# Attention scores straight from q and k: one float32 matmul per block of queries in place of three matmuls of parts

## The chip, the cores and the metric

The kernel runs on one core of a Trainium2 chip, for one layer of a transformer-like encoder block over 256 tokens of width 2048. A core has a matrix engine (PE in the profile, with its weight loads listed apart as PEld), a vector engine (DVE), a scalar engine (ACT), a general engine (POOL), and a queue engine that issues most transfers (SP). The metric is the device time of one execution in microseconds (us), lower is better. A difference of about 0.2% is the least that a measurement of this kernel tells from no change.

## The reference, cut to what matters

The whole block is computed: RMSNorm, one input projection, windowed attention beside a Fourier mixer, output projection, a gated feed-forward part and a final RMSNorm. Only the attention's scores are touched by the change. For each of the 12 query heads (three share one key head) they are

```python
scores = jnp.einsum('bnqkgd,bnskd->bnkgqs', qb, kb).astype(jnp.float32)
scores = scores * (HEAD_DIM ** -0.5)
...
scores = scores + alibi[None, None]
scores = jnp.where(valid[None, :, None, None], scores, NEG_INF)
...
m = jnp.maximum(jnp.max(scores, axis=-1, keepdims=True), sink_b)
p = jnp.exp(scores - m)
```

The sequence has 256 positions and the window reaches 128 either way, so for one head the kernel forms the whole 256 x 256 table of scores, as two blocks of 128 queries against 256 keys, with a contraction over the 128 elements of a head.

## The kernel before, in words

All big products are done on numbers in a reduced float32 format (float32r, "F32R" in the code). To keep float32 accuracy an operand is split in two parts: `hi` is the operand rounded to that format (a copy on ACT), and `lo` is the remainder (a subtraction on DVE). A product is then three matmuls that add up in one accumulator: hi by hi, hi by lo, lo by hi. A matmul with plain float32 operands (tiles of type "F32") needs no split. The kernel has a few of those before the change: the warm-up matmuls `ps_warm`, the Fourier channel products `ps_y` (L652, matrices `G` by columns `uf`, 129 and 127 columns each), and four transposes `ps_t`.

The program is written out in order by hand: an engine does its instructions in the order in which the code issues them, with no reordering by a planner. The middle part of it, the stretch from 58 to 163 us of the profile, has 16 units, one for each head of `QK_ORDER` (k0, q0, q1, q2, k1, q3 and so on). A unit's own work is 32 matmuls of line L372 (`still_weights`) that make one head of q or k, transposed, from the weights and the activations `hT`. Around it the dictionaries `before`, `beside` and `behind` hang the small steps of earlier heads, by the distance to a head's own unit: one unit later its projection is read out (`qk_out`, then `qk_parts`), two units later `scores` puts its matmuls on PE ahead of that unit's projection and `scores_out` and `exps` follow on DVE and ACT, and further on the weights of the softmax are applied, turned and multiplied with v (`values`, L842). On DVE and ACT the small steps stand ahead of the split of a later unit's weight tile: L197 (`hi`, ACT, 1.9 us) and L205 (`lo`, DVE, 2.2 us), which a matmul needs two units later.

The steps that the change touches:

- `qk_out` copies half of the accumulator out (ACT, `tmp_q` or `tmp_k`, L725) and adds the other half (DVE, `add_q` or `add_k`, L727). For a key it also multiplies by `r1b`, the normalizing factor of each token (DVE, L729).
- `qk_parts` makes the operands of the scores. For a key: `kT`'s high part on ACT (L737) and low part on DVE (L738). For a query: both parts by `split_scaled`, with a scale that holds the head's slope (ACT L298, DVE L299).
- `scores` issues three matmuls of 256 columns for each of the two query blocks, L748, into one bank `ps_s`.

`ps_*` are accumulator banks, `kT` and `qT` the transposed keys and queries in on-chip memory. `scores` runs for all 12 query heads.

Of the kernel before, what the change touches and what calls it, by code (L numbers as in the profile page):

```python
# [8 lines left out]
F32 = mybir.dt.float32  # L9
F32R = mybir.dt.float32r  # L10
AF = mybir.ActivationFunctionType
ALU = mybir.AluOpType

P = 128
D = 2048
S = 256
# [41 lines left out]
def slopes():  # L58
    def pow2(n):
        start = 2.0 ** (-8.0 / n)  # L60
        return [start ** (i + 1) for i in range(n)]

    return pow2(8) + pow2(16)[0::2][: NH - 8]
# [57 lines left out]
def block_kernel(  # L121
# [19 lines left out]
    nc = tc.nc  # L141
    SL = slopes()
# [6 lines left out]
    def f32(ap):  # L149
        return ap.bitcast(F32)  # L150

    def bank(pool, name):
        return pool.tile([P, 512], F32, tag=pool.name, name=name)
# [92 lines left out]
    def u_part(k, o, n, m=1):  # L246

        rows = ux[k // 4][:, (k < 4) * U_HEAD :].rearrange("p (k c) -> p k c", k=4)
        return rows[:, k % 4 : k % 4 + m, o : o + n]
# [39 lines left out]
    ps = bank(dn, "ps_warm")  # L289
# [6 lines left out]
    def split_scaled(dst, src, g):  # L296

        nc.scalar.activation(dst[:, 0:S], src, AF.Copy, scale=g)  # L298
        nc.vector.scalar_tensor_tensor(  # L299
            dst[:, S : 2 * S], src, g, f32(dst[:, 0:S]), ALU.mult, ALU.subtract  # L300
        )
# [105 lines left out]
    for c in range(4):  # L407
        t = base.tile([P, 4, 512], F32R, tag=f"hT{c}", name=f"hT{c}")
        hT.append(t)
    ps_u = [bank(mm, f"ps_u{b}") for b in range(2)]  # L410
    for k in range(NK):
# [3 lines left out]
        n = 1 if c < 2 else 2  # L415
# [3 lines left out]
        if q % n == 0:  # L419
            w, h = u_part(k, 0, FW, n), hi[:, q : q + n, :]  # L420
# [3 lines left out]
        if k < 4:  # L424

            for p, w in enumerate([hi, hi, lo]):
                for b in range(2):
# [3 lines left out]
                        start=k == 0 and p == 0, stop=False,  # L431
# [9 lines left out]
    ph = pa.enter_context(tc.tile_pool(name="pa", bufs=1))  # L441
# [78 lines left out]
    r1b = ph.tile([P, S], F32, tag="r1b", name="r1b")  # L520
# [202 lines left out]
    def qk_out(kind, h, ps):  # L723
        tmp = ph.tile([P, S], F32, tag="tmp", name=f"tmp_{kind}{h}", bufs=2)
        nc.scalar.activation(tmp, ps[:, S : 2 * S], AF.Copy)  # L725
        add = ph.tile([P, S], F32, tag="add", name=f"add_{kind}{h}", bufs=2)
        nc.vector.tensor_tensor(add, ps[:, 0:S], tmp, ALU.add)  # L727
        if kind == "k":
            nc.vector.tensor_tensor(add, add, r1b, ALU.mult)  # L729
        st["add", kind, h] = add  # L730

    def qk_parts(kind, h):

        add = st.pop(("add", kind, h))
        t = ph.tile([P, 512], F32R, tag=f"{kind}T", name=f"{kind}T{h}", bufs=2)
        if kind == "k":
            nc.scalar.activation(t[:, 0:S], add, AF.Copy)  # L737
            nc.vector.tensor_tensor(t[:, S : 2 * S], add, f32(t[:, 0:S]), ALU.subtract)  # L738
        else:
            split_scaled(t, add, -1.0 / float(SL[h]))  # L740
        qk_sb[kind, h] = t

    def scores(h):
        ps = st["s", h] = bank(dn, f"ps_s{h}")
        qT, kT = qk_sb.pop(("q", h)), qk_sb["k", h // GQA]
        for b in range(2):
            for n, (qo, ko) in enumerate([(0, 0), (0, S), (S, 0)]):
                nc.tensor.matmul(  # L748
                    ps[:, b * S : (b + 1) * S],
                    qT[:, qo + b * P : qo + (b + 1) * P],  # L750
                    kT[:, ko : ko + S],
                    start=n == 0,
                    stop=n == 2,
                )

    def scores_out(h):

# [100 lines left out]
    for i in range(N_QK, N_OUT + 8):  # L858
        heads = {i - s: h for (kind, h), s in slot_of.items() if kind == "q"}
        new = [kh for kh, s in slot_of.items() if i - s == 1]  # L860
        for n, h in sorted(heads.items()):
            if n == values_at(h):
                at(before, i, values, h)
        if 4 in heads and heads[4] not in FLIPS:
            at(before, i, turn, heads[4])
        if 2 in heads:
            at(before, i, scores, heads[2])
        for kind, h in new:
            at(beside, i, lambda k=kind, h=h: qk_out(k, h, st.pop(("ps", k, h))))
        for n, h in sorted(heads.items()):  # L870
            if n == values_at(h) - 1 and h in FLIPS:
                at(beside, i, flip_parts, h)
        for kind, h in new:
            at(beside, i, qk_parts, kind, h)
        for n, h in sorted(heads.items()):
            if n == values_at(h):
                at(beside, i, values_out, h)
        if 3 in heads:
            at(beside, i, weigh, heads[3])
            if heads[3] in FLIPS:  # L880
                at(beside, i, flip_out, heads[3])
        if 4 in heads:
            at(beside, i, flip_in if heads[4] in FLIPS else turn_out, heads[4])
        if 2 in heads:
            at(beside, i, scores_out, heads[2])
        if 2 in heads:
            at(behind, i, exps, heads[2])
# [68 lines left out]
    for n, (c, kq) in enumerate(OUT_ORDER):  # L956
# [15 lines left out]
        if kq >= 2:  # L972
            part = "a" if kq == 2 else "f"
            ps = ps_a[c] if kq < 3 else ps_a[c, "f"]
# [345 lines left out]
    for q in range(OPEN):  # L1320
        kind, j = items[q]
        ps = bank(mm, f"ps_{kind}{j}")
# [29 lines left out]
    for n, it in enumerate(items):  # L1352
# [8 lines left out]
        if it[0] in ("gate", "val"):  # L1361
            kind, j = it
            ps = bank(mm, f"ps_{kind}{j}")
# [4 lines left out]
        if it[0] == "product":  # L1368
            kind, g, c, p = it
# [3 lines left out]
            elif end and p in ("P2", "N4"):  # L1373
                ps = joined[c, p] = bank(mm, f"ps_{p}{g}{c}")
                by_parts(ps, parts[p], *halves.pop(it), GROUPS[g][1], True, False)
            else:
                ps = bank(mm, f"ps_{p}{g}{c}")
# [5 lines left out]
        else:  # L1383
            kind, c = it
            hi, lo = halves.pop(up_index[n])
            if c < 2:
                ps = [joined.pop((c, p)) for p in ("P2", "N4")]
            else:
                ps = [bank(mm, f"ps_l{c}{b}") for b in range(2)]
# [172 lines left out]
```

## Time and profile before

| what | value |
|---|---|
| median of 3 runs | 933.79 us (933.52 to 934.1) |
| the profiled execution, its own time | 933.83 us |
| its span in the profile | 932.1 us |
| granted PE clock, mean | 0.998 |
| PE busy in the span | 923.2 us, 99% |
| DVE busy | 776.2 us, 83% |
| ACT busy | 543.6 us, 58% |

A row of a group names line, engine, operation and tiles (out<-in), the shape (partitions x elements), and a count; then the busy time and the mean duration of one. Matmuls overlap: one of 512 columns is listed with 389 ns, but the next one begins 0.23 us after it. So busy times of matmuls cannot be added up as time of the span. What can be added up is the chain that ended last: its pieces touch each other, so the length of a piece is what it takes of the span. A timeline row gives start and length of an instruction, or of several of one kind in a row ("x6"), from the first's start to the last's end.

### The profile page before, as it was taken

The page shows a single profiled execution, that of the slowest core. Times are in us where ns is not written, and L with a number is a line of the kernel's source. Part 1 is how long each engine was busy: PE and PEld are TensorE (multiplying, and loading weights), DVE is VectorE, ACT ScalarE, POOL GpSimd, SP SyncE. Part 2 cuts the span into 40 slices and gives each one's busy share as a digit, 9 for nine tenths or more (in the row PEclk, how much of TensorE's full clock was granted, in tenths as well). Part 3 has the DMA queues.
Part 4 walks back from the last instruction along what each step waited for, and adds up shares of the span by engine and source line. Part 5 has one row for each costly group of instructions (what it writes and reads, how often), then busy time and mean ns, then how long its engine had stood idle before and what let it go on. Part 6 is the DMA issues. An engine that isn't in the chain of part 4 may idle for free.

```text
span 932.1 us, 12883 instructions
## 1 busy us (share of the span) xinstructions
PE 923.2 (99%) x4973; PEld 799.9 (86%) x4973; DVE 776.2 (83%) x997; ACT 543.6 (58%) x689; POOL 62.8 (7%) x79
## 2 busy tenths in 40 slices
PE   9999999999999999999999999999999999999996
PEld 7888998888888888888888888888888888888885
DVE  7768998787768877898877997888978789989995
ACT  6756777546465655565555665555755556655553
POOL 0101111200000000000000000000000000000002
PEclk9999999999999999999999999999999999999999
DMA  9865777667777668788797769887787968779652
GB/s 361 331 225 158 249 241 215 201 198 269 230 274 256 203 207 256 242 274 263 229 299 251 240 209 298 223 260 233 268 240 244 306 221 269 237 238 272 203 180 91
DMA packets 59597, 225.16 MB, mean 242 GB/s; under 512 B 24465, under 2 KB 30225, under 8 KB 35984
## 3 DMA queue, kind: packets, MB, share of 16 engines
q1 hardware_dynamic: 54928, 194.72, 57.9%
q0 software_dynamic: 4464, 29.36, 17.0%
q8 instruction: 39, 0.64, 0.3%
q10 hardware_dynamic: 144, 0.26, 0.1%
q14 instruction: 22, 0.18, 0.0%
HBM read 216.98 MB, written 7.08 MB: 240 GB/s over the span
## 4 chain that ended last, share of the span: by engine, by line
PE 98%; DMA 0%; ACT 0%; DVE 0%; issue 0%; POOLq 0%; POOL 0%; ACTq 0%
PE ps_gate L372 25%; PE ps_val L372 25%; PE ps_q L372 7%; PE ps_P L1233 4%; PE ps_P L1234 4%; PE ps_P L1232 3%; PE ps_N L1233 3%; PE ps_N L1234 3%; PE ps_N L1232 3%; PE ps_k L372 2%; PE ps_a L357 2%; PE ps_a L355 2%; PE ps_a L356 2%; PE ps_s L748 1%; PE ps_o L842 1%; PE ps_ff L355 1%
## 5 line engine op out<-in xcount | busy, mean ns | idle before, releaser
L205 DVE TENSOR_TENSOR lo<-raw,hi 128x2048 fp32r<-128x2048 f32 (+2 forms) x133 | 295.0, 2221 | 28.3 <-ACT hi L197 28.0
L197 ACT ACTIVATE hi<-raw 128x2048 fp32r<-128x2048 f32 (+1 forms) x131 | 246.8, 1887 | 27.6 <-PE ps_a L356 10.8
L372 PE MATMUL ps_gate<-hU,hi 128*128 128x512 f32 x688 | 236.1, 389 | 0.0
L372 PE MATMUL ps_val<-hU,hi 128*128 128x512 f32 x688 | 236.1, 389 | 0.0
L372 PE MATMUL ps_gate<-hU,lo 128*128 128x256 f32 x688 | 189.9, 276 | 0.0
L372 PE MATMUL ps_val<-hU,lo 128*128 128x256 f32 x687 | 189.6, 276 | 0.0
L372 PEld LDWEIGHTS ps_gate<-hU,hi 128*128 128x128 f32 x688 | 129.2, 188 | 26.8
L372 PEld LDWEIGHTS ps_val<-hU,hi 128*128 128x128 f32 x688 | 129.2, 188 | 26.8
L372 PEld LDWEIGHTS ps_gate<-hU,lo 128*128 128x128 f32 x688 | 129.2, 188 | 1.3
L372 PEld LDWEIGHTS ps_val<-hU,lo 128*128 128x128 f32 x687 | 129.0, 188 | 1.3
L1013 ACT ACTIVATE ft_g<-ps_gate 128x256 f32<-128x256 f32 x43 | 16.5, 384 | 121.1 <-PE ps_gate L372 121.1
L1013 ACT ACTIVATE ft_v<-ps_val 128x256 f32<-128x256 f32 x43 | 16.5, 383 | 87.0 <-PE ps_val L372 87.0
L372 PE MATMUL ps_q<-hT,hi 128*128 128x512 f32 x192 | 65.0, 391 | 0.0
L1232 PE MATMUL ps_P<-hi_P,op_P 128*128 128x512 f32 x144 | 56.0, 389 | 0.0
L1233 PE MATMUL ps_P<-hi_P,op_P 128*128 128x512 f32 x144 | 56.0, 389 | 0.0
L1234 PE MATMUL ps_P<-lo_P,op_P 128*128 128x512 f32 x144 | 56.0, 389 | 0.0
L372 PE MATMUL ps_q<-hT,lo 128*128 128x256 f32 x192 | 51.2, 277 | 0.0
L1130 DVE TENSOR_TENSOR lo_N<-sumw,hi_N 128x2048 fp32r<-128x2048 f32 (+1 forms) x20 | 41.5, 2076 | 9.4 <-ACT hi_N L1129 9.2
L1232 PE MATMUL ps_N<-hi_N,op_N 128*128 128x512 f32 x108 | 42.0, 389 | 0.0
L1233 PE MATMUL ps_N<-hi_N,op_N 128*128 128x512 f32 x108 | 42.0, 389 | 0.0
L1234 PE MATMUL ps_N<-lo_N,op_N 128*128 128x512 f32 x108 | 42.0, 389 | 0.0
L372 PEld LDWEIGHTS ps_q<-hT,hi 128*128 128x128 f32 x192 | 35.2, 188 | 6.6
(415 smaller groups left out, 1592.4 us busy)
## 6 DMA issues: line engine op xcount, KB each, us to landing
raw<-in_w_up SPq DMA_DIRECT2D x86, 1024.0 KB, 6.6
raw<-in_w_in SPq DMA_DIRECT2D x20, 1024.0 KB, 5.4
raw<-in_w_out SPq DMA_DIRECT2D x16, 1024.0 KB, 5.1
sumw<-in_w_down POOLq DMA_DIRECT2D x16, 1024.0 KB, 8.6
raw<-in_w_down_late SPq DMA_DIRECT2D x4, 1024.0 KB, 6.8
raw<-in_w_down_last SPq DMA_DIRECT2D x4, 768.0 KB, 4.0
turnp<-flip SPq DMA_DIRECT2D x44, 64.0 KB, 1.9
flop<-turnp SPq DMA_DIRECT2D x11, 256.0 KB, 3.9
```

What stands on the lines that cost most here:

```text
L197: nc.scalar.activation(halves[i][0][:, s], raws[i][:, s], AF.Copy)
L205: nc.vector.tensor_tensor(lo[:, s], raws[i][:, s], f32(hi[:, s]), ALU.subtract)
L355: nc.tensor.matmul(ps, ah, wh, start=first and q == q0, stop=False)
L356: nc.tensor.matmul(ps, al, wh, start=False, stop=False)
L357: nc.tensor.matmul(ps, ah, wl, start=False, stop=last and q == q0 + len(kk) - 1)
L372: nc.tensor.matmul(ps[:, x], (hi, lo)[i][:, k * P : (k + 1) * P], hk(k)[:, x], start=n == 0 and k == 0, stop=n == len(order) - 1 and k == ...
L748: nc.tensor.matmul(ps[:, b * S : (b + 1) * S], qT[:, qo + b * P : qo + (b + 1) * P], kT[:, ko : ko + S], start=n == 0, stop=n == 2,)
L1013: nc.scalar.activation(tmp, ps[:, S : 2 * S], AF.Copy)
L1130: nc.vector.tensor_tensor(lo, src, f32(hi), ALU.subtract)
L1232: nc.tensor.matmul(ps, o[:, 0, p, :], hi[:, s], start=first and p == 0, stop=False)
L1233: nc.tensor.matmul(ps, o[:, 1, p, :], hi[:, s], start=False, stop=False)
L1234: nc.tensor.matmul(ps, o[:, 0, p, :], lo[:, s], start=False, stop=last and p == n - 1)
```

## The change

The high and low parts of q and k go. `qk_parts` now writes one plain float32 tile `t` of 256 columns: for a key it is the product of `add` with `r1b`, which stood in `qk_out` before (DVE, new line L735), and for a query it is `add` times the same scale as before (ACT, new line L737). `scores` issues one float32 matmul for each block of 128 queries in place of three float32r matmuls, new line L744. The results go to the same bank in the same shape, and nothing behind `scores` changes.

```diff
         add = ph.tile([P, S], F32, tag="add", name=f"add_{kind}{h}", bufs=2)
         nc.vector.tensor_tensor(add, ps[:, 0:S], tmp, ALU.add)
+        st["add", kind, h] = add
+
+    def qk_parts(kind, h):
+
+        add = st.pop(("add", kind, h))
+        t = ph.tile([P, 512], F32, tag=f"{kind}T", name=f"{kind}T{h}", bufs=2)[:, 0:S]
         if kind == "k":
-            nc.vector.tensor_tensor(add, add, r1b, ALU.mult)
-        st["add", kind, h] = add
-
-    def qk_parts(kind, h):
-
-        add = st.pop(("add", kind, h))
-        t = ph.tile([P, 512], F32R, tag=f"{kind}T", name=f"{kind}T{h}", bufs=2)
-        if kind == "k":
-            nc.scalar.activation(t[:, 0:S], add, AF.Copy)
-            nc.vector.tensor_tensor(t[:, S : 2 * S], add, f32(t[:, 0:S]), ALU.subtract)
+            nc.vector.tensor_tensor(t, add, r1b, ALU.mult)
         else:
-            split_scaled(t, add, -1.0 / float(SL[h]))
+            nc.scalar.activation(t, add, AF.Copy, scale=-1.0 / float(SL[h]))
         qk_sb[kind, h] = t
...
         for b in range(2):
-            for n, (qo, ko) in enumerate([(0, 0), (0, S), (S, 0)]):
-                nc.tensor.matmul(
-                    ps[:, b * S : (b + 1) * S],
-                    qT[:, qo + b * P : qo + (b + 1) * P],
-                    kT[:, ko : ko + S],
-                    start=n == 0,
-                    stop=n == 2,
-                )
+            nc.tensor.matmul(
+                ps[:, b * S : (b + 1) * S], qT[:, b * P : (b + 1) * P], kT, start=True, stop=True
+            )
```

On PE the scores of head 0 stand between the projection of head 2 (`ps_q`) and a Fourier product (`ps_y`). Before:

```order
L372 MATMUL ps_q_656<-hT_140,hi_566 128x512
L372 MATMUL ps_q_656<-hT_140,lo_567 128x256 x2
L748 MATMUL ps_s_719<-kT_644,qT_703 128x256 x6
L652 MATMUL ps_y_726<-uf_635,G_76 128x129
L652 MATMUL ps_y_726<-uf_635,G_77 128x127
L372 MATMUL ps_q_729<-hT_137,hi_647 128x512 x2
```

and after:

```order
L372 MATMUL ps_q_654<-hT_140,hi_566 128x512
L372 MATMUL ps_q_654<-hT_140,lo_567 128x256 x2
L744 MATMUL ps_s_716<-kT_643,qT_701 128x256 x2
L652 MATMUL ps_y_719<-uf_635,G_76 128x129
L652 MATMUL ps_y_719<-uf_635,G_77 128x127
L372 MATMUL ps_q_722<-hT_137,hi_645 128x512 x2
```

Six instructions of 256 columns became two of the same width, at the same place among the others.

On DVE the one step that moves is the multiplication of a key by `r1b`. Here it is for the third key head, beside the parts `pt` of the softmax weights of an earlier head (`flip_parts`). Before:

```order
L205 TENSOR_TENSOR lo_1201<-raw_971,hi_1200 128x2048
L727 TENSOR_TENSOR add_k_1261<-ps_k_1134,tmp_k_1259 128x256
L729 TENSOR_TENSOR add_k_1261<-add_k_1261,r1b 128x256
L833 TENSOR_TENSOR pt_1265<-flop_1100,pt_1264 128x256 x2
L738 TENSOR_TENSOR kT_1270<-add_k_1261,kT_1270 128x256
L299 SCALAR_TENSOR_TENSOR cat_1273<-ps_o_1212,vec,cat_1273 128x256
```

and after:

```order
L205 TENSOR_TENSOR lo_1171<-raw_952,hi_1170 128x2048
L727 TENSOR_TENSOR add_k_1227<-ps_k_1105,tmp_k_1225 128x256
L825 TENSOR_TENSOR pt_1230<-flop_1075,pt_1229 128x256 x2
L735 TENSOR_TENSOR kT_1235<-add_k_1227,r1b 128x256
L299 SCALAR_TENSOR_TENSOR cat_1237<-ps_o_1182,vec,cat_1237 128x256
```

The multiplication went behind the two subtractions of `pt`, to the place where the subtraction for `kT`'s low part stood, and that subtraction is gone. No transfer is issued at another place than before.

## The prediction

> **What bounds the kernel now.** The page comes first: its busy times, and then the chain that ended last.
>
> ```profile
> span 932.1 us, 12883 instructions
> ...
> PE 923.2 (99%) x4973; PEld 799.9 (86%) x4973; DVE 776.2 (83%) x997; ACT 543.6 (58%) x689; POOL 62.8 (7%) x79
> ...
> PE 98%; DMA 0%; ACT 0%; DVE 0%; issue 0%; POOLq 0%; POOL 0%; ACTq 0%
> ```
>
> PE carries 98% of the chain. DVE has 83% too, so the next question is whether PE ever waits for it. The view of waits, for PE over the whole span, has two rows, both at the start:
>
> ```profile
> PE ps_warm L291 <- POOL ones L283: 1.0, 1, 1.0
> PE ps_u L429 <- ACT hT L298: 0.2, 1, 0.2
> ```
>
> The stretch of the change agrees. In the table by stretches PE is busy in all 105 us of it:
>
> ```profile
> 58.00:163.00 105.00, 105.00 (x649) 94.27 (x648) 91.02 (x200) 72.94 (x158) 16.77 (x21) 1.00 0.69 213
> ```
>
> (The columns after the length are PE, PEld, DVE, ACT, POOL; then the granted clock, here 1.00.) So in this stretch a microsecond off PE is a microsecond off the span, and a microsecond off DVE or ACT is worth nothing by itself. Since no later wait of PE appears either, nothing behind the stretch can absorb a shift: weights that come from memory are already there when PE wants them. The time is PE's stream and a fixed tail.
>
> **What the scores cost now.** The chain in order of time gives what each group of matmuls takes of the span:
>
> ```profile
> 64.10 5.47 PE ps_q L372 x32
> 69.57 0.72 PE ps_s L748 x6
> 70.29 0.44 PE ps_y L652 x4
> 70.73 5.46 PE ps_q L372 x32
> 76.19 0.72 PE ps_s L748 x6
> 76.91 0.44 PE ps_y L652 x4
> ...
> 101.81 0.72 PE ps_s L748 x6
> ```
>
> A head's six score matmuls take 0.72 us, 0.12 each, wherever they stand. Twelve heads: 12 x 0.72 = 8.64 us. All of that is on the path and is replaced.
>
> **What a plain float32 matmul costs.** The same view shows it, in `ps_y`. The program has two instructions there for each Fourier group, the profile has four matmuls and as many weight loads. The rows by tile, for `ps_y`, for `ps_f` (float32r, of nearly the same width), and for the scores:
>
> ```profile
> L652 PEld LDWEIGHTS ps_y<-uf,G x16: 188/190/192, 63.4 to 83.6; 128*128 128x128 f32 x16
> L652 PE MATMUL ps_y<-uf,G x16: 271/273/274, 63.5 to 83.7; 128*128 128x129 f32 x8, 128*128 128x127 f32 x8
> ...
> L631 PE MATMUL ps_f<-pos_s,u_lo x4: 223/225/230, 56.2 to 57.7; 128*128 128x130 f32 x4
> ...
> L748 PE MATMUL ps_s<-kT,qT x72: 279/283/287, 69.4 to 161.5; 128*128 128x256 f32 x72
> ```
>
> Eight instructions, 16 records: a plain float32 matmul is done in two passes, each with a load of its own. And a pass of 128 columns lasts 273 ns, where a float32r matmul of 130 columns lasts 225 and one of 256 lasts 283. Per column a pass seems to go at half the rate of float32r. Two instructions of 128 columns take 0.44 us of the chain, so an instruction of 256 columns should take twice what one of 128 does: 2 x 0.22 = 0.44 us, and a head's two of them 0.88 us.
>
> Bounds for that 0.88. Above: if a pass of 256 columns at half rate costs what float32r takes for 512 columns, the piece of the chain late in the kernel is
>
> ```profile
> 914.95 0.23 PE ps_e L1411
> ```
>
> and four passes are 4 x 0.23 = 0.92 us. Below: what a matmul pays once, whatever its length, is saved when two short passes become a long one. 512 columns take 0.23 against 2 x 0.12 for two matmuls of 256, so that is about 0.01 a pass, and 0.88 - 4 x 0.01 = 0.84 us. I take 0.88, since `ps_y` is the same kind of operation; 0.84 and 0.92 come from float32r rows.
>
> The Trainium skill has two sentences on this. "FP8 and Floating Point Precision" (TensorE Precision Notes) says that true float32 takes four passes through the array, a product of highs and lows each. "Perfetto Trace Analysis" (Engine Utilization) halves the array's rate for the float32 mode with low and high halves. Two records at half rate are four passes, so page and trace agree, and both speak against the change: four passes of 256 columns in place of three, hence by the rule a third more than the array's share of 0.72 us, or about 0.96 us a head as an estimate from that page and the row. Nothing below rests on this.
>
> **The change, part by part.**
>
> PE: 12 x (0.88 - 0.72) = +1.92 us, all on the path. The six weight loads a head become four (one a pass); they overlap, as the PEld rows of `ps_y` do, and longer passes hide them better.
>
> DVE loses 12 low parts of queries and 4 of keys; ACT loses 4 high parts of keys. The groups:
>
> ```profile
> L299 DVE SCALAR_TENSOR_TENSOR qT<-add_q,qT 128x256 fp32r<-128x256 f32 x12 | 5.1, 422 | 2.9 <-ACT qT L298 2.9
> L738 DVE TENSOR_TENSOR kT<-add_k,kT 128x256 fp32r<-128x256 f32 x4 | 1.7, 422 | 1.0 <-ACT kT L737 1.0
> L737 ACT ACTIVATE kT<-add_k 128x256 fp32r<-128x256 f32 x4 | 1.7, 418 | 4.0 <-DVE add_k L729 4.0
> ```
>
> That is 5.1 + 1.7 = 6.8 us of DVE and up to 3.9 us of its waits, and 1.7 us of ACT with 4.0 of its waits. It frees the splits behind them earlier, which PE doesn't wait for: 0 on the path.
>
> The key's multiplication moves behind two `pt` subtractions of 0.42 us on DVE. ACT no longer reads its result, PE does, and the first scores with this key stand at least a whole unit later, 5.47 us of the chain. Cost 0. The queries' operand is ready when ACT has written it, without DVE's half. The tightest place before is head 3:
>
> ```profile
> 93.63 0.42 DVE L299 SCALAR_TENSOR_TENSOR qT<-add_q,qT 128x256 fp32r<-128x256 f32 x1 [0.48 <-ACT qT L298]
> ...
> 94.73 0.28 PE L748 MATMUL ps_s<-kT,qT 128*128 128x256 f32 x1
> ```
>
> The low part is done at 94.05, 0.68 us ahead of PE; without it ACT's copy ends some 0.45 us sooner still. No new wait, cost 0. Tail and transfers: 0, since both follow PE at the same distance.
>
> Sum: 933.83 + 1.92 = 935.75 us for the profiled execution, which lies 0.04 above the median of the runs, within their scatter of 0.6 us. I forecast **935.8 us**, 0.2% slower. The bounds make 933.8 + 12 x 0.12 = 935.2 and 933.8 + 12 x 0.20 = 936.2.
>
> **The rivals.**
>
> *Full-rate passes: faster.* Passes of `ps_y` follow each other at 0.11 us, which may be set by the loads and not by the columns:
>
> ```profile
> 70.00 0.53 PEld L652 LDWEIGHTS ps_y<-uf,G 128*128 128x128 f32 x4
> ```
>
> Four loads of 0.19 span 0.53, one each 0.11. If columns go at float32r's rate, a pass of 256 costs 0.12, as in the scores now, and a head 4 x 0.12 = 0.48: 12 x (0.48 - 0.72) = -2.88, 930.9 us. It decides if four passes take under 0.72, that is 0.18 each. Against it stands the pass's 273 ns, not 225; but the profile's ends of matmuls are modelled and a duration can hold a wait for a load, so the pitch of 0.11 alone can't exclude it. The skill's "TensorE: Matmul & The Clock Gate" (LDWEIGHTS) puts a load of 128 columns at 107 ns, which fits this reading of the pitch as well as the other.
>
> *Loads in the open: much slower.* If a float32 pass of this width let no load run beside it, each would pay 0.11 more: 12 x (0.88 + 0.44 - 0.72) = +7.7, 941.5 us. Against it: in `ps_y` loads overlap passes already, or four couldn't take 0.44.
>
> *Freed DVE time is worth something.* 6.8 us fewer on DVE would count if PE waited for it. The two rows of waits exclude it: the gain is 0, and with half-rate passes the time is the forecast's.
>
> **How the numbers follow.** Half-rate passes: 0.92. There the difference goes from +1.4 to +2.4 us, and 0.2% of 933.8 is 1.87 us, which a head reaches at 0.72 + 0.156 = 0.876 us. The middle, 0.88, lies just above that; of 0.84 to 0.92 the upper half goes with `ps_y` itself and with the 512-column row, so I give slower 0.66 and within the bound 0.26 of these. Full-rate passes: 0.05, faster. Open loads: 0.02, slower. Something that cancels the change: 0.01, same. Together faster 0.05, same 0.27, slower 0.68. The range, with the runs' scatter of 0.3 us to either side of the bounds, is 935.0 to 936.6 us; it leaves out the two priced rivals and the cancelled case, with 0.08.
>
> **What the changed profile would show.** Right: `ps_s` with 48 records, two loads and two passes for each instruction, each pass 0.22 us of the chain and listed with some 385 ns, 0.88 us a head; DVE's busy time 6.8 us lower; no new row among PE's waits; span near 934.0. Wrong: passes at 0.12 with a load as what they wait for (full rate), or loads that begin only when a pass has ended (open loads), or a row of PE waiting for `qT` or `kT`. If passes take 0.21, the mechanism is right and the difference falls below what a measurement can tell.

## The result, and the profile after

| | before | after |
|---|---|---|
| median, 19 runs each | 933.79 us | 935.41 us |
| span of the profiled execution | 932.1 us | 933.5 us |
| PE busy | 923.2 us | 924.6 us |
| DVE busy | 776.2 us | 770.9 us |

The ratio of after to before is 1.0017, with a 95% interval from 1.001 to 1.0025: the change makes the kernel 1.6 us slower, and the interval leaves no change out. That is a shade under the 0.2% that the prediction took as the least a measurement can tell. Some executions, of the kernel before and of several variants, take some 15 us longer for a reason that was not found; the comparisons leave them out, and where an experiment has no other execution, only its rows early in the kernel are read.

PE still has 98% of the chain, and its waits in the changed kernel are the two of before:

```profile
PE ps_warm L291 <- POOL ones L283: 1.0, 1, 1.0
PE ps_u L429 <- ACT hT L298: 0.2, 1, 0.2
```

The chain in order of time, at the same place as in the prediction (start, length, piece):

```profile
63.76 5.47 PE ps_q L372 x32
69.23 0.86 PE ps_s L744 x4
70.09 0.44 PE ps_y L652 x4
70.54 5.46 PE ps_q L372 x32
```

The scores of a head, four matmuls now, take 0.86 us in place of 0.72, and the pieces around them are unchanged. 12 x (0.86 - 0.72) = 1.7 us, which accounts for the whole difference of 1.6. The scores' rows by tile, with the one DVE row that makes the keys:

```profile
L744 PEld LDWEIGHTS ps_s<-kT,qT x48: 187/189/192, 69.0 to 162.6; 128*128 128x128 f32 x48
L744 PE MATMUL ps_s<-kT,qT x48: 377/379/381, 69.1 to 162.8; 128*128 128x256 f32 x48
L735 DVE TENSOR_TENSOR kT<-add_k,r1b x4: 425/946/975, 59.9 to 136.4; 128x256 f32<-128x256 f32 x4
```

24 instructions, 48 loads and 48 matmuls: two passes each. The multiplication of a key, 0.42 us before, is listed with over 0.9 us in most of its four places. DVE's busy time fell by 5.3 us and not by the 6.8 of the dropped subtractions; four such multiplications of 0.82 us in the mean in place of 0.42 add 1.6 us, which accounts for the 1.5 between.

### The profile page after: what moved, and what is told of

The parts are those of the page before. It is cut to its first block, busy times and chain, and to the rows that moved or that the text cites. A ratio compares the mean times of both kernels' runs of the same rounds, so it can differ in the third digit from the quotient of the medians.

```text
span 933.5 us, 12818 instructions
## 1 busy us (share of the span) xinstructions
PE 924.6 (99%) x4949; PEld 799.5 (86%) x4949; DVE 770.9 (83%) x981; ACT 542.7 (58%) x685; POOL 62.3 (7%) x79
## 4 chain that ended last, share of the span: by engine, by line
PE 98%; DMA 0%; ACT 0%; DVE 0%; issue 0%; POOLq 0%; POOL 0%; ACTq 0%
PE ps_gate L372 25%; PE ps_val L372 25%; PE ps_q L372 7%; PE ps_P L1225 3%; PE ps_P L1226 3%; PE ps_P L1224 3%; PE ps_N L1225 3%; PE ps_N L1226 3%; PE ps_N L1224 3%; PE ps_k L372 2%; PE ps_a L357 2%; PE ps_a L355 2%; PE ps_a L356 2%; PE ps_s L744 1%; PE ps_o L834 1%; PE ps_ff L355 1%
```

## The experiments

The theory: PE's stream alone sets the time; a float32 matmul is two passes, each set by its columns at half of float32r's rate, 0.86 us a head; relief of DVE and ACT is worth nothing. The rivals: the relief is worth something and the matmuls cost more than the total shows; or the loads set a pass and not the columns.

### The dropped split work put back

```diff
         if kind == "k":
             nc.vector.tensor_tensor(t, add, r1b, ALU.mult)
+            nc.scalar.activation(rest, t, AF.Copy)
+            nc.vector.tensor_tensor(rest, t, rest, ALU.subtract)
         else:
-            nc.scalar.activation(t, add, AF.Copy, scale=-1.0 / float(SL[h]))
+            g = -1.0 / float(SL[h])
+            nc.scalar.activation(t, add, AF.Copy, scale=g)
+            nc.vector.scalar_tensor_tensor(rest, add, g, t, ALU.mult, ALU.subtract)
```

(`rest` is the other half of the operand's tile, which is 512 columns wide.)

> The changed kernel with the dropped split work put back (ACT's copy for each key, DVE's subtraction for each query and key, written where nothing reads them); PE's matmuls are those of the changed kernel. Theory (PE's stream alone sets the time, 0.86 us a head): the 6.8 us of DVE and 1.7 us of ACT come back and cost nothing, 935.4 us, within 0.3 of the changed kernel, 1.6 above the kernel before. Rival (the change won time on DVE and ACT and lost more on PE): slower than the changed kernel by a part of 6.8 us, 936 to 942.

Measured: 935.5 us, ratio to before 1.0018 (1.0009 to 1.0027), against 1.0017 of the changed kernel. DVE and ACT carry what they carried in the kernel before, and PE's scores are still 0.86 us a head:

```profile
PE 924.9 (99%) x4949; PEld 800.5 (86%) x4949; DVE 776.0 (83%) x997; ACT 543.6 (58%) x689; POOL 62.5 (7%) x79
...
95.27 0.86 PE ps_s L749 x4
```

The median lies 0.1 us from that of the changed kernel, and PE's view of waits has one row, `ps_warm` at the start. So of the 6.8 us at most a few tenths could have come back: within what these runs tell, the work that the change saves on DVE and ACT is worth nothing here.

### Before, without low parts, with the same number of matmuls

```diff
-            for n, (qo, ko) in enumerate([(0, 0), (0, S), (S, 0)]):
+            for n in range(3):
                 nc.tensor.matmul(
-                    ps[:, b * S : (b + 1) * S],
-                    qT[:, qo + b * P : qo + (b + 1) * P],
-                    kT[:, ko : ko + S],
-                    start=n == 0,
-                    stop=n == 2,
+                    ps[:, b * S : (b + 1) * S], qT[:, b * P : (b + 1) * P], kT[:, 0:S],
+                    start=True, stop=True,
                 )
```

(The low parts are no longer made.)

> The kernel before without its low parts of q and k: the DVE work of 16 subtractions is gone (6.8 us), PE still does six float32r matmuls a head, each of the high parts, each overwriting the last. It leaves out the low parts of the scores. Theory (PE alone): the time of before, 933.8 within 0.3; six matmuls still take 0.72 us a head. Rival (DVE relief is worth something): faster than before by a part of 6.8 us.

Its runs scatter, from 933.4 to 936.5 us, and the ratio is 1.0012 (1.0002 to 1.0022). The runs of before that were taken beside it span as much, but of them 2 in 25 lie above 934.5, and here 5 in 7. So the time was not the 933.8 expected to within 0.3, and why these runs lie higher stays open. A gain, which the rival needs, is excluded by the interval. In the profiled execution (934.0 us, span 932.2) DVE is busy 6.8 us less and the chain reads like that of before:

```profile
PE 923.2 (99%) x4973; PEld 799.6 (86%) x4973; DVE 769.4 (83%) x981; ACT 543.2 (58%) x689; POOL 62.3 (7%) x79
...
69.43 0.72 PE ps_s L747 x6
```

### One float32r matmul for each block of queries

The same, with `range(1)` in place of `range(3)`.

> The kernel before with the high parts alone and one float32r matmul for each block of queries: two a head. It leaves out the low parts of the scores. Theory (each 0.12 us of PE is 0.12 us of the time): 12 x (0.24 - 0.72) = -5.8, 928.0 us within 0.5. Rival (something late in the kernel, such as weights from memory, absorbs a shift of PE): less than half of that, 931 or more.

Measured: 929.2 us, ratio 0.9951 (0.9938 to 0.9964), 4.7 us below before and not 5.8. The scores did what was expected (0.24 us for the two matmuls of a head). The missing microsecond shows among PE's waits, where two new rows stand:

```profile
PE ps_o L838 <- DVE pt L829: 0.8, 1, 0.8
PE ps_t L793 <- DVE sc L786: 0.4, 1, 0.4
```

They lie behind the last heads' scores, in the chain in order of time:

```profile
164.59 0.17 DVE varf L574
164.76 0.07 issue
164.83 1.67 POOL sums_f L575
...
167.77 0.76 DVE pt L829 x2
168.53 0.40 DVE cat L299
168.93 0.09 DVE ex L783
169.01 0.02 issue
169.04 0.37 DVE sc L786
169.41 0.14 issue
169.54 0.72 PE ps_t L793 x4
```

Once PE is 5.8 us shorter in this stage, it reaches the last heads' products before DVE has their weights. Ahead of these on DVE stands the sum for the Fourier group's norm (`total_scale`), which itself waits for a slow POOL instruction of 1.67 us. 5.8 - 1.2 = 4.6 us. So "nothing behind the stretch absorbs a shift" holds for a longer PE, and for a shorter one only up to where this chain takes over. The rival's 931 us or more did not come either.

### The float32 matmuls in pieces of 64 columns

```diff
-            nc.tensor.matmul(
-                ps[:, b * S : (b + 1) * S], qT[:, b * P : (b + 1) * P], kT, start=True, stop=True
-            )
+            for c in range(0, S, 64):
+                nc.tensor.matmul(
+                    ps[:, b * S + c : b * S + c + 64], qT[:, b * P : (b + 1) * P],
+                    kT[:, c : c + 64], start=True, stop=True,
+                )
```

> The changed kernel with each float32 matmul of 256 columns cut into four of 64 columns: 16 passes a head of 64 columns each, with a weight load for each, in place of 4 passes of 256. The columns streamed are the same. If only the columns counted (0.84 ns a column and pass, 0.215 / 256), a pass would take 0.054 and the time stay near 935.4. If a load can't take less than some 0.11, a pass takes 0.11 and a head 1.76: 12 x (1.76 - 0.86) = +10.8, 946.2 us. I expect the second; it says from which width on a float32 pass is set by its columns: 0.11 / 0.84 ns = 131 columns.

Measured: 947.1 us, ratio 1.0141 (1.0119 to 1.0163). Rows by tile and the chain:

```profile
L745 PEld LDWEIGHTS ps_s<-kT,qT x192: 187/192/192, 69.6 to 174.5; 128*128 128x128 f32 x192
L745 PE MATMUL ps_s<-kT,qT x192: 217/275/275, 69.7 to 174.5; 128*128 128x64 f32 x192
...
98.40 1.73 PE ps_s L745 x16
```

16 passes in 1.73 us are 0.11 each, though they have a quarter of the columns: here something other than the columns sets the pass. The load is the nearest reading, since the loads too follow each other at 0.11. But every pass here has a load of its own, so the run can't tell it from another fixed cost of a pass. The time is 0.9 us above the 946.2 expected. The scores account for 12 x (1.73 - 0.86) = 10.4 us of the 11.7 between this kernel and the changed one. In the profiled executions another 0.6 us lies ahead of the first scores (69.85 against 69.23 us), where the two kernels do the same, and 0.2 us in the three `ps_y` behind scores (0.50 each in place of 0.44); the remaining 0.5 stays open.

The listed duration, 275 ns for 64 columns, is that of `ps_y` with 128 (273). So it doesn't follow the columns, and the 273 ns that the prediction read as a sign of half-rate columns was no such sign. The spacing of 0.11 in `ps_y` is none either, since 64 columns have it too. What shows the columns' rate is the changed kernel itself: 0.215 us for 256 columns, twice the 0.11 of a narrow pass. That is 0.84 ns a column, where float32r takes 0.227 us for 512 columns late in the kernel before (`ps_e`), 0.44 ns a column. No float32 pass wider than 256 columns was run, so the rate rests on this one width.

### Float32r with as many column steps

```diff
-            for n, (qo, ko) in enumerate([(0, 0), (0, S), (S, 0)]):
+            for n in range(2):
                 nc.tensor.matmul(
-                    ps[:, b * S : (b + 1) * S],
-                    qT[:, qo + b * P : qo + (b + 1) * P],
-                    kT[:, ko : ko + S],
-                    start=n == 0,
-                    stop=n == 2,
+                    ps, qT[:, n * S + b * P : n * S + (b + 1) * P], kT, start=True, stop=True
                 )
```

> The kernel before with four float32r matmuls of 512 columns a head (high and low part of the keys side by side, once with the query's high and once with its low part), each over the whole bank and overwriting the last. It leaves out the sum of the products, so the scores are not those of the reference. It has as many column steps as four float32 passes of 256 columns at two steps a column, if that is how they work. If both take the same: 0.215 each, 0.86 a head, 935.4. If float32r keeps the 0.227 that it takes elsewhere in this kernel: 0.91 a head, 12 x (0.91 - 0.72) = +2.3, 936.1. I expect the second.

The second run reads the key's high part twice, with `kT[:, 0:S].unsqueeze(1).broadcast_to([P, 2, S])` as the moving operand:

> As the run with four float32r matmuls of 512 columns, but the 512 columns are the key's high part read twice (256 columns, then the same again). It leaves out the low part of the keys and the sum of the products. If the 0.227 of float32r for 512 columns comes from reading 512 different columns: 0.215 here. If it comes from the format: 0.227, as with 512 different ones. I expect the second.

Each ran once. Of the first (953.0 us) only the early chain is read; the second took 936.3 us. Both spend the same on a head, here the one with different columns and then the one with repeated ones:

```profile
95.72 0.93 PE ps_s L748 x4
```

```profile
95.17 0.93 PE ps_s L748 x4
```

0.93 / 4 = 0.233 us a matmul, whichever columns it reads: 12 x (0.93 - 0.72) = 2.5 us, and the second one's time, 2.6 above before, agrees. It is more than the 0.227 expected, and 8% more than a float32 pass that makes as many steps (0.215), if that makes two a column. Reading 512 different columns is not the reason; what is was not found. It may not be these matmuls alone: in both runs three of the projections that follow scores, whose code is that of before, take 5.60 us in place of 5.46. They too are some 3% slower, at a granted clock of 1.00.

### The key's multiplication at its old place

```diff
+        if kind == "k":
+            t = ph.tile([P, 512], F32, tag="kT", name=f"kT{h}", bufs=2)[:, 0:S]
+            nc.vector.tensor_tensor(t, add, r1b, ALU.mult)
+            qk_sb[kind, h] = t
+            return
         st["add", kind, h] = add
```

(This stands in `qk_out`; `qk_parts` does nothing for a key.)

> The changed kernel with the key's multiplication where it stood before, ahead of the two pt subtractions on DVE. In the changed kernel three of the four are listed with 0.95 to 0.97 us in place of 0.42, at the moment POOL adds sq_a. Theory: at the old place all four take 0.42 us again, DVE is busy some 1.6 us less, and the time stays at 935.4 within 0.3, since PE doesn't wait for it. Rival (the long multiplication costs time further on): faster than the changed kernel by up to 1.6 us.

Measured: 935.4 us, ratio 1.0016 (1.0007 to 1.0025): the time of the changed kernel, as expected. Of the multiplications one in four is still long, so the expectation of four short ones missed:

```profile
L730 DVE TENSOR_TENSOR kT<-add_k,r1b x4: 424/425/903, 60.0 to 136.6; 128x256 f32<-128x256 f32 x4
```

The slow spot moved instead. In the changed kernel the multiplications of the third and fourth key ran beside POOL's addition of `sq_a`; at the old place the two `pt` subtractions behind them do. The second key's runs beside the same addition for the Fourier part (`sq_f`) in both kernels, with no `pt` next to it, and so it stays long. Here are DVE and POOL for the third key in the changed kernel, then for the fourth in this run:

```profile
109.83 0.97 DVE L735 TENSOR_TENSOR kT<-add_k,r1b 128x256 f32<-128x256 f32 x1
...
109.75 0.77 POOL L554 TENSOR_TENSOR sq_a<-sq_a,sq 128x256 f32<-128x256 f32 x1 [1.17 <-ACT sq L550]
```

```profile
136.95 1.31 DVE L829 TENSOR_TENSOR pt<-flop,pt 128x256 fp32r<-128x256 f32 x2
...
137.07 0.90 POOL L554 TENSOR_TENSOR sq_a<-sq_a,sq 128x256 f32<-128x256 f32 x1 [1.17 <-DVE kT L730]
```

Two subtractions that took 0.75 us together take 1.31 where POOL's addition runs beside them, for both keys. DVE's busy time is 771.2 us, against 770.9 in the changed kernel: the cost went from one instruction to its neighbours. PE waits for neither.

## Why the prediction was right, and where its terms were off

- **What bounds the kernel.** Right. PE's two rows of waits are the same after the change, and the run with the split work put back (935.5 us) shows DVE's and ACT's relief to be worth nothing.
- **PE's term, +1.92 us.** That PE's longer stream is the cost is shown; the size was a little high: 0.86 us a head where 0.88 was taken, thus 1.7 us. The passes are 0.215 each and not 0.22. The row `ps_y` that I doubled holds passes of 0.11, which is what any narrow pass takes; at 256 columns that floor is passed, and what remains is the columns. The estimate of 0.96 us a head, a third above 0.72, was 0.10 too high: the six float32r matmuls take 0.47 ns a column, the float32 passes 0.42 a step if they make two steps a column.
- **The evidence for half rate.** The conclusion held, but neither of the two rows behind it supports it. The listed 273 ns against 225 doesn't follow the columns, as the pieces of 64 columns show with 275, and the doubled 0.11 is what a pass of 64 columns takes too. It was luck that the doubling came so near: 128 columns at 0.84 ns make 0.108 us, almost exactly the floor of 0.11. The prediction named this weakness under the faster rival and still gave that rival 0.05; by the rows of before alone it deserved more.
- **The bound of 0.2%.** The forecast of 935.8 lay 0.39 above the measured 935.41, and the measured 0.17% falls just inside the bound, to which the text gave 0.27 and to the slower side 0.68. So the likelier of its answers is not the one that came, though the time lies inside the range. The interval of the comparison was narrower than the bound, so that a change of this size could be told from none.
- **Loads in the open.** Did not happen: the chain has 0.215 a pass, loads included. Its sum in the prediction is off: 12 x (0.88 + 0.44 - 0.72) is +7.2 and not +7.7, so 941.0 us. The range, too, is 934.9 to 936.5 us when 0.3 is put to either side of the bounds. Neither slip changes the forecast.
- **The moved multiplication, 0.** Right for the time. That it would meet POOL and take 0.9 us was not seen, and so DVE's busy time fell by 5.3 us and not by the 6.8 named as a sign. The kernel before has one such meeting: two `pt` subtractions at 175.86 us take 1.30 us in place of 0.75, beside POOL's `sq_a`.
- **No new wait.** Right. Shortening PE would have made one, as the run with one matmul a block shows.

## What to carry to other kernels

Where one engine never waits, cost a change by that engine's start-to-start spacing alone: six float32r matmuls of 0.12 were cheaper than four float32 passes of 0.215, and 6.8 us of work saved elsewhere bought nothing. Read the rate of a matmul from the chain, not from listed durations, and only at a width at which its columns surely take longer than the least time of a pass (0.11 us here). Before counting on a gain from a shorter bounding engine, look for the chain that would come next.

## What the runs showed that was not expected

- A float32 pass over 256 columns takes 0.215 us, a float32r matmul over 512 columns 0.227 in the rest of this kernel (in the chain of before six of them, `ps_e`, go from 914.05 to 915.41 us) and 0.233 in place of the scores, with repeated columns too. If both make 512 steps, float32r is some 5 to 8% slower per step.
- A float32 pass of 64 columns took 0.11 us, as one of 128 did. An estimate of the width from which the columns count is 131 (0.11 us over 0.84 ns a column); no width between 128 and 256 was run.
- Two passes are not the rule for every matmul with float32 operands: the four transposes `ps_t` of the kernel before leave four records, one each, and take 0.44 us of the chain together.
- A DVE instruction with both inputs in on-chip memory takes 0.9 us in place of 0.42 while POOL adds two tiles of that size. The Trainium skill, "SBUF — State Buffer" (SBUF: two separate sides), says that such a DVE operation and a POOL operation that reads the same memory take a shared pair of ports in turn, each for its whole length. The trace agrees in that DVE is held up: POOL's addition ends 0.69 us after DVE's start (109.75 + 0.77 - 109.83), and DVE's multiplication 0.28 us later. That DVE stood still for all of the 0.69 is not borne out: its own 0.42 would not fit in the 0.28 behind, as far as POOL's listed end can be trusted.
